# Streamed tiles at 96 and 224 instead of 64 bytes behind the weights, and down projections in written order

## The chip, the cores and the metric

The kernel runs on one core of a Trainium2 chip. The metric is the device time of one execution in microseconds (us). Engines are named as the profile names them: PE multiplies matrices, PEld is its loading of weights, DVE, ACT and POOL work on tiles, SP issues the transfers.

## What is computed

A decoder trunk over 512 tokens of width 1024: two layers, each a mixer and a gated convolutional feed-forward network, with an RMS norm ahead of each and one at the end. The first mixer is dilated window attention (three groups of eight heads), the second a Mamba-2 scan.

```python
for i in range(DEPTH):                       # 2
    h = rmsnorm(x, mix_norm_w[i])
    x = x + (dilated_attention_mixer(h, ...) if i % 2 == 0 else ssd_mixer(h, ...))
    h = rmsnorm(x, ffn_norm_w[i])
    x = x + conv_ffn(h, ffn_w_up[i], ffn_conv_w[i], ffn_conv_b[i], ffn_w_down[i])
return rmsnorm(x, final_norm_w)

def conv_ffn(h, w_up, conv_w, conv_b, w_down):
    u = causal_depthwise_conv(h @ w_up, conv_w, conv_b)
    gate, up = u[..., :D_FF], u[..., D_FF:]           # 2816 each
    return (jax.nn.silu(gate) * up) @ w_down
```

## The kernel before

Activations lie transposed: a tile has 128 features on the partitions and the 512 tokens along the free dimension, so it takes 2048 bytes of each partition. Every dense product is split in two parts for accuracy. A value's high part is the value cast to float32r, its low part what is left. `mm3` (L131) then does three matmuls for one block of 128 x 128 weights: high weights with the high activations, high weights with the low activations, low weights with the high activations. Each is a weight load of 128 columns (512 bytes of each partition) and a stream of 512 columns. The stream does not run straight through its tile: `in_turns` (L122) reads four values (16 bytes), steps 64 bytes on, does so 32 times, and makes four such turns.

A weight unit is 128 x 1024 values: `load_unit` (L106) fetches it into `raw`, ACT casts it to `hi`, and DVE (POOL for the z tiles) subtracts to get `lo`. The buffers of `hi` and `lo` hold 1088 values, which is 4352 bytes or 17 times 256, so all of them begin at the same place modulo 256 bytes. So do the blocks in them, 512 bytes apart, and the streamed tiles, 2048 bytes apart. One number therefore says how the streamed operand lies to the loaded one: the distance of their first bytes modulo 256. The filler tiles `gap` and `gap2`, which nothing uses, set it. It is 64 for each of the 6,504 matmuls with 512 streamed columns and for the 288 with 256.

The streamed tiles are `xh0` to `xh7` and `xl0` to `xl7` (the normed activations), and those that `high_low` makes: attention outputs `o..`, gated units `g..`, scan outputs `y..`. `high_low` takes both parts from one ring of 16 buffers (tag `hl`). For the values of the attention groups 1 and 2 (`v_steps`) the roles are swapped: blocks of `xh` and `xl` are loaded as weights and the weight unit is streamed. There `load_unit` puts the unit 32 values (128 bytes) into its buffer (`at=32`), which again makes the distance 64.

A scheduler orders the instructions of each engine by a timing model of its own, except inside `tc.manual_schedule`, where the written order stands. The mixer of the second layer is written out by hand for PE. The feed-forward network (`ffn`) was left to the scheduler: in three parts (8, 8 and 6 blocks of 128 hidden units) it projects up, gates, and then projects down through `down` (L215), which makes eight output blocks `wd..0` to `wd..7`, each a sum over the part's 8 or 6 gated tiles. `down` writes the product with the last gated tile later than the others (`held`, `finish`), since that tile is made last. Sums lie in three PSUM banks (`mm_bank`), so a fourth block waits until DVE has added the first to the residual `xr`. In the very last part `finish` (L953) works on halves of 256 tokens (`wz..`), norms, and writes the result through output tiles `ot`, which come from the `hl` ring too.

Of the kernel before, what the change touches and what calls it, by code (L numbers as in the profile page):

```python
# [9 lines left out]
F32 = mybir.dt.float32  # L10
F32R = mybir.dt.float32r
# [3 lines left out]
P = 128  # L15
S = 512
D = 1024
KD = D // P
# [33 lines left out]
def trunk(ctx: ExitStack, tc: tile.TileContext, A, out):  # L52
# [4 lines left out]
    cp = ctx.enter_context(tc.tile_pool(name="cp", bufs=1))  # L57
    wr = ctx.enter_context(tc.tile_pool(name="wr", bufs=4))
    wh = ctx.enter_context(tc.tile_pool(name="wh", bufs=5))
    k2 = ctx.enter_context(tc.tile_pool(name="k2", bufs=2))  # L60
# [15 lines left out]
    def t2(name, tag, bufs, pool=k2, dtype=F32):  # L76
        return pool.tile([P, 512], dtype, tag=tag, name=name, bufs=bufs)

    def high_low(name):

        return t2(f"{name}h", "hl", 16, dtype=F32R), t2(f"{name}l", "hl", 16, dtype=F32R)


    par = cp.tile([P, C_END], F32, tag="par", name="par")
# [5 lines left out]

    rcol = cp.tile([P, 4], F32, tag="rcol", name="rcol")
    xh = [cp.tile([P, S], F32R, tag=f"xh{k}", name=f"xh{k}") for k in range(KD)]
    xl = [cp.tile([P, S], F32R, tag=f"xl{k}", name=f"xl{k}") for k in range(KD)]
    rbc = cp.tile([P, S], F32, tag="rbc", name="rbc")

    cp.tile([P, 48], F32, tag="gap", name="gap")
    k2.tile([P, 16], F32, tag="gap2", name="gap2", bufs=1)
    dma(par[:, :C_FFN], A["par"][:, :C_FFN])
    V.memset(ones, 1.0)
    V.memset(mhalf, -0.5)  # L100
# [8 lines left out]
    def load_unit(src, name, n=1024, pieces=1, low=V, at=0):  # L109
        raw = wr.tile([P, 1024], F32, tag="raw", name=f"raw_{name}")  # L110
        hi, lo = (wh.tile([P, 1088], F32R, tag=t, name=f"{t}_{name}")[:, at : at + 1024] for t in ("hi", "lo"))
        for i in range(pieces):
            s = slice(i * n // pieces, (i + 1) * n // pieces)
            dma(raw[:, s], src[:, s])
            if i < pieces - 1:
                V.tensor_copy(hi[:, s], raw[:, s])
            else:
                SC.copy(hi[:, s], raw[:, s])  # L118
            low.tensor_tensor(lo[:, s], raw[:, s], hi.bitcast(F32)[:, s], op=ALU.subtract)  # L119
        return hi, lo  # L120
# [5 lines left out]
    def long_product(dst, w, x, first, last):  # L126
        T.matmul(in_turns(dst), w, in_turns(x), start=first, stop=last)  # L127

    def mm3(dst, hi, lo, at, rh, rl, first, last):
        w_h = hi[:, at * P : (at + 1) * P]  # L130
        w_l = lo[:, at * P : (at + 1) * P]  # L131
        long_product(dst, w_h, rh, first, False)
        long_product(dst, w_h, rl, False, False)
        long_product(dst, w_l, rh, False, last)
# [77 lines left out]
            )  # L212
        return p

    def down(n, load, ms, operand, kn, done, width=512, depth=1):  # L215

        held = []

        def finish():
            m, p, hi, lo, at = held.pop(0)  # L220
            mm3(p, hi, lo, at + kn - 1, *operand(kn - 1), kn == 1, True)
            done(m, p)

        for m in ms:
            hi, lo, at = load(m)
            p = mm_bank(f"{n}{m}")[:, :width]
            for c in range(kn - 1):
                mm3(p, hi, lo, at + c, *operand(c), c == 0, False)
            if len(held) == depth:
                finish()  # L230
            held.append((m, p, hi, lo, at))
        while held:
            finish()
# [4 lines left out]
    def v_steps(g, half, pieces=1):  # L238

        state = {}  # L240
        n = f"v{g}{half}"

        def load(u):
            if u not in state:
                state[u] = load_unit(A["wv"][((g - 1) * 2 + half) * 4 + u], f"{n}{u}", pieces=pieces, at=32)
            return state[u]

        def step(u, bs=(0, 1)):
            if u == 0:
                state["p"] = [mm_bank(f"{n}{j}") for j in range(3)] + [aux_bank(f"{n}3")]  # L250
            hi, lo = load(u)
            for j in range(4):
                js = slice(j * P, (j + 1) * P)
                for b in bs:
                    k = 2 * u + b
                    cs = slice(b * 512, (b + 1) * 512)
                    p = state["p"][j]
                    long_product(p, xh[k][:, js], hi[:, cs], k == 0, False)
                    long_product(p, xl[k][:, js], hi[:, cs], False, False)
                    long_product(p, xh[k][:, js], lo[:, cs], False, k == KD - 1)  # L260
            if u == 3 and bs[-1]:
                tiles = []
                for j in range(4):
                    v = t2(f"{n}_{j}", "v", 12, s3)
                    SC.activation(v, state["p"][j], AF.Copy, scale=rcol[:, j : j + 1])
                    tiles.append(v)
                vt[g, half] = tiles

        return load, [lambda *bs, u=u: step(u, *bs) for u in range(4)]
# [3 lines left out]
    load, first = v_steps(1, 0, 2)  # L273
# [260 lines left out]
    def ffn(layer, done):  # L534
        for part, (c0, cn) in enumerate(FF_PARTS):
            gh, gl = [], []
            for c in range(c0, c0 + cn):
                ab = []
                for gu in range(2):
                    i = 2 * c + gu  # L540
                    n = f"u{layer}_{i}"
                    p = project(A["wup"][layer * 44 + i], n)
                    us = t2("us" + n, "us", 3, lp)
                    V.tensor_tensor(us, p, rbc, op=ALU.mult)  # L544
                    a = t2("a" + n, "a", 13, lp)
                    conv(a, us, C_FCW + (layer * 44 + i) * 3, C_FCB + layer * 44 + i, 3)
                    ab.append(a)
                SC.activation(ab[0], ab[0], AF.Silu)

                by = V if layer == 1 and c == NFF - 1 else G  # L550
                by.tensor_tensor(ab[1], ab[0], ab[1], op=ALU.mult)  # L551
                g_h, g_l = high_low(f"g{c}")
                SC.copy(g_h, ab[1])
                by.tensor_tensor(g_l, ab[1], g_h.bitcast(F32), op=ALU.subtract)
                gh.append(g_h)
                gl.append(g_l)
            n = cn * P

            def load(m):
                i = (layer * len(FF_PARTS) + part) * KD + m  # L560
                return (*load_unit(A["wdn"][i][:, :n], f"wd{i}", n), 0)

            def add(m, p):
                V.tensor_tensor(xr[m], xr[m], p, op=ALU.add)  # L564
                if part == len(FF_PARTS) - 1:
                    done(m)

            if layer == 1 and part == len(FF_PARTS) - 1:
                finish(load, lambda c: (gh[c], gl[c]), cn)
                return  # L570
            down(f"wd{layer}{part}", load, range(KD), lambda c: (gh[c], gl[c]), cn, add)

    def up_first(layer):
        return [(A["wup"][layer * 44 + i], f"u{layer}_{i}") for i in range(3)]
# [383 lines left out]
    def finish(load, operand, cn):  # L958
        for hf in range(2):
            ts = slice(hf * 256, (hf + 1) * 256)  # L960
            ssum = t2(f"ssum4{hf}", "ssum", 2)[:, 0:256]
            last = {}

            def add(m, p):
                x = xr[m][:, ts]
                V.tensor_tensor(x, x, p, op=ALU.add)
                if m < KD - 1:
                    square(m, x, ssum)
                else:
                    last["sq"] = t2("sq", "sq", 2)[:, 0:256]  # L970
                    SC.activation(last["sq"], x, AF.Square)
                w = t2(f"xw{m}", "a", 13, lp)[:, 0:256]
                SC.activation(w, x, AF.Copy, scale=col(C_FIN + m))
                last[m] = w

            down(f"wz{hf}", load, range(KD), lambda c: [t[:, ts] for t in operand(c)], cn, add, 256, 2 - hf)
            rc = sm.tile([P, 2], F32, tag="rc", name="rc", bufs=2)
            inv_rms(ssum, D, rc, last["sq"])
            p = along_free(rc, "rb")[:, 0:256]
            SC.copy(rbc[:, ts], p)  # L980
            for k in range(0, KD, 2):
                ot = t2("ot", "hl", 16)
                for i in range(2):
                    o = ot[:, i * 256 : (i + 1) * 256]
                    if k + i in (1, 4, 7):
                        G.tensor_tensor(o, last[k + i], rbc[:, ts], op=ALU.mult)
                    else:
                        V.tensor_tensor(o, last[k + i], p, op=ALU.mult)
                queue = nc.sync if k % 4 == 0 else nc.scalar
                queue.dma_start(out[k : k + 2, :, ts].rearrange("k p t -> p k t"), ot.rearrange("p (k t) -> p k t", k=2))  # L990
# [103 lines left out]
```

## Time and profile before

| | |
|---|---|
| Median of three runs | 1667.94 us (1667.35 to 1669.39) |
| The profiled execution | 1668.99 us |
| its span, first to last instruction | 1667.2 us |
| Granted clock of PE over the span | 0.998 |
| Matmuls with 512 streamed columns | 6,504 of 8,230 records |
| Weights fetched, HBM read in all | 162.01 MB |

The span is what the views of the trace cover; 1.8 us of the execution lie outside it. A matmul's record (384 ns in the mean for those of the up projections) overlaps the next one's, so how fast a row of matmuls goes is read from the chain of waits instead: it gives, in order of time, stretches of one kind of work with their length and count, and length over count is the spacing. The view by windows gives each engine's busy time in a stage.

### The profile page before, as it was taken

How to read it: one execution, taken by the hardware profiler on the slowest of the kernel's cores; microseconds unless marked ns; L12 is line 12 of the kernel's file. 1: busy time of each engine (PE TensorE's matmuls, PEld its weight loads, DVE VectorE, ACT ScalarE, POOL GpSimd, SP SyncE). 2: the span in 40 equal slices, each digit the busy share in tenths (PEclk: the TensorE clock that was granted, in tenths of full speed). 3: DMA queues.
4: the chain of work that ended last, by engine and by line, in shares of the span. 5: the costliest groups of instructions: out<-in, count | busy, mean ns of one | idle time of the engine just before them, and what ended most of it. 6: DMA issues, size and time to landing. Idle time of an engine off the chain costs nothing.

```text
span 1667.2 us, 21490 instructions
## 1 busy us (share of the span) xinstructions
PE 1648.6 (99%) x8230; PEld 1400.2 (84%) x8230; DVE 1072.1 (64%) x1796; ACT 665.4 (40%) x1000; POOL 464.3 (28%) x303
## 2 busy tenths in 40 slices
PE   9999999999999999999999999999989999999997
PEld 8888888888888888888888888888878888888887
DVE  5366555366658745745666888887787684574565
ACT  5233332333244423433445545454443542342345
POOL 0443443144404210220232232333230331121023
PEclk9999999999999999999999999999999999999999
DMA  7322222222223323233233333322332232332323
GB/s 252 102 77 75 82 84 89 89 76 89 76 89 127 101 88 114 90 100 101 76 114 116 102 101 102 114 75 103 101 102 78 87 113 88 102 101 89 110 74 120
DMA packets 52342, 165.56 MB, mean 99 GB/s; under 512 B 5840, under 2 KB 8144, under 8 KB 52240
## 3 DMA queue, kind: packets, MB, share of 16 engines
q1 hardware_dynamic: 51152, 163.15, 29.6%
q8 instruction: 65, 1.06, 0.3%
q10 hardware_dynamic: 1088, 1.05, 0.2%
q14 instruction: 37, 0.30, 0.1%
HBM read 162.01 MB, written 2.16 MB: 98 GB/s over the span
## 4 chain that ended last, share of the span: by engine, by line
PE 87%; DVE 7%; ACT 3%; issue 2%; DMA 1%; POOL 0%; SPq 0%; POOLq 0%; ACTq 0%; DVEq 0%
PE u L127 28%; PE qk L127 15%; PE wd L127 12%; PE v L127 8%; PE wso L127 4%; PE z L127 3%; PE xs L127 3%; PE wz L127 2%; PE wo L127 2%; DVE axs L529 1%; PE b L127 1%; PE c L127 1%; PE pp L416 1%; PE pg L429 1%; PE po L424 1%
## 5 line engine op out<-in xcount | busy, mean ns | idle before, releaser
L127 PE MATMUL u<-xl,hi_u 128*128 128x512 f32 x704 | 270.0, 384 | 0.4 <-DVE xl L176 0.4
L127 PE MATMUL u<-xh,hi_u 128*128 128x512 f32 x704 | 270.4, 384 | 0.0
L127 PE MATMUL u<-xh,lo_u 128*128 128x512 f32 x704 | 270.0, 384 | 0.0
L551 POOL TENSOR_TENSOR au<-au,au 128x512 f32<-128x512 f32 x43 | 56.7, 1320 | 427.0 <-DVE au L529 406.4
L118 ACT CAST hi_u<-raw_u 128x1024 fp32r<-128x1024 f32 x88 | 91.1, 1043 | 193.9 <-PE u L127 102.1
L529 DVE SCALAR_TENSOR_TENSOR au<-usu,par,au 128x510 f32<-128x510 f32 (+1 forms) x176 | 160.8, 918 | 5.9 <-ACT au L527 1.0
L331 POOL TENSOR_TENSOR rotqk<-rotqk,sr 32x512 f32<-32x512 f32 x48 | 91.9, 1914 | 258.1 <-DVE rotqk L330 215.0
L127 PEld LDWEIGHTS u<-xl,hi_u 128*128 128x128 f32 x704 | 131.9, 187 | 25.9 <-DVE xl L176 0.8
L127 PEld LDWEIGHTS u<-xh,lo_u 128*128 128x128 f32 x704 | 131.9, 187 | 25.4
L127 PEld LDWEIGHTS u<-xh,hi_u 128*128 128x128 f32 x704 | 131.9, 187 | 25.2
L127 PE MATMUL qk<-xh,hi_qk 128*128 128x512 f32 x384 | 149.3, 389 | 0.0
L127 PE MATMUL qk<-xl,hi_qk 128*128 128x512 f32 x384 | 148.4, 387 | 0.0
L127 PE MATMUL qk<-xh,lo_qk 128*128 128x512 f32 x384 | 147.2, 383 | 0.0
L544 DVE TENSOR_TENSOR usu<-u,rbc 128x512 f32<-128x512 f32 x88 | 60.5, 690 | 113.3 <-PE u L127 103.9
L119 DVE TENSOR_TENSOR lo_u<-raw_u,hi_u 128x1024 fp32r<-128x1024 f32 x88 | 110.8, 1264 | 24.2 <-ACT hi_u L118 24.2
L564 DVE TENSOR_TENSOR xr<-xr,wd 128x512 f32<-128x512 f32 x40 | 27.3, 687 | 116.8 <-PE wd L127 116.8
L327 DVE TENSOR_TENSOR qk<-qk,cr 128x512 f32<-128x512 f32 x48 | 33.0, 688 | 91.5 <-PE qk L127 91.3
L118 ACT CAST hi_qk<-raw_qk 128x1024 fp32r<-128x1024 f32 x48 | 50.2, 1045 | 100.4 <-PE v L127 50.0
L127 PEld LDWEIGHTS qk<-xh,lo_qk 128*128 128x128 f32 x384 | 72.0, 187 | 13.4
L127 PEld LDWEIGHTS qk<-xh,hi_qk 128*128 128x128 f32 x384 | 72.0, 188 | 13.0
L118 ACT CAST hi_wd<-raw_wd 128x1024 fp32r<-128x1024 f32 (+1 forms) x56 | 52.3, 952 | 76.7 <-PE wd L127 39.7
L127 PEld LDWEIGHTS qk<-xl,hi_qk 128*128 128x128 f32 x384 | 72.1, 188 | 12.5
(636 smaller groups left out, 3931.1 us busy)
## 6 DMA issues: line engine op xcount, KB each, us to landing
raw_u<-in_wup SPq DMA_DIRECT2D x88, 512.0 KB, 3.2
raw_qk<-in_wqk SPq DMA_DIRECT2D x48, 512.0 KB, 3.2
raw_wd<-in_wdn SPq DMA_DIRECT2D x32, 512.0 KB, 3.2
raw_wd<-in_wdn SPq DMA_DIRECT2D x24, 384.0 KB, 2.9
raw_xs<-in_win SPq DMA_DIRECT2D x16, 512.0 KB, 3.3
raw_z<-in_win SPq DMA_DIRECT2D x16, 512.0 KB, 3.6
lm<-rows SPq DMA_DIRECT2D x32, 256.0 KB, 5.9
raw_wso<-in_wso SPq DMA_DIRECT2D x16, 512.0 KB, 3.2
```

Source lines behind the costliest of these rows:

```text
L118: SC.copy(hi[:, s], raw[:, s])
L119: low.tensor_tensor(lo[:, s], raw[:, s], hi.bitcast(F32)[:, s], op=ALU.subtract)
L127: T.matmul(in_turns(dst), w, in_turns(x), start=first, stop=last)
L327: V.tensor_tensor(at(t), of(p), of(cr), op=ALU.mult)
L331: G.tensor_tensor(rot[R, :], rot[R, :], sr[R, :], op=ALU.mult)
L416: T.transpose(pp[:, b * P : (b + 1) * P], pr[:, b * P : (b + 1) * P], ident)
L424: T.matmul(po[:, ii], v0[h][:, b * P : (b + 1) * P], pts[i][:, (b - i + 1) * P : (b - i + 2) * P], start=b == max(i - 1, 0), stop=b == i,)
L429: T.matmul(pg[:, ii], vt[g, half][i][:, es], pts[i][:, (g + 1) * P : (g + 2) * P], start=g == 1, stop=g == 2,)
L529: V.scalar_tensor_tensor(dst[:, j:], src[:, : S - j], col(c_w + taps - 1 - j), dst[:, j:], op0=ALU.mult, op1=ALU.add,)
L544: V.tensor_tensor(us, p, rbc, op=ALU.mult)
L551: by.tensor_tensor(ab[1], ab[0], ab[1], op=ALU.mult)
L564: V.tensor_tensor(xr[m], xr[m], p, op=ALU.add)
```

## The change

Four edits go together.

Places. A filler of 128 bytes (`gap1`) is put between `xh7` and `xl0`. `gap` shrinks from 192 to 32 bytes and `gap2` grows from 64 to 96. `high_low` now has two rings of 8 buffers, `high` and `low`, and a filler of 128 bytes (`gap3`) is made between them when it is first called. Worked out from these sizes, a streamed high part is now 96 bytes and a streamed low part 224 bytes behind the loaded weights modulo 256: 4,336 of the 6,504 matmuls have 96, and 2,168 have 224. Tiles of the other pools move by multiples of 32 bytes, among them the operands of transposes (from 192 to 64 modulo 256).

Values. Their weight unit begins 48 instead of 32 values into its buffer (192 bytes), which gives 96 against blocks of `xh` and 224 against blocks of `xl`.

Order. Down projections other than the very last part are inside `manual_schedule` for PE. `down` has a new switch `late`: the first two blocks' last products come when the third block has done three of its own tiles.

Outputs. `ot` comes from the ring `high`, so from 8 buffers in place of 16.

```diff
+    kept = []
     def high_low(name):
-        return t2(f"{name}h", "hl", 16, dtype=F32R), t2(f"{name}l", "hl", 16, dtype=F32R)
+        high = t2(f"{name}h", "high", 8, dtype=F32R)
+        if not kept:
+            k2.tile([P, 32], F32, tag="gap3", name="gap3", bufs=1)
+        kept.append(name)
+        return high, t2(f"{name}l", "low", 8, dtype=F32R)
...
     xh = [cp.tile([P, S], F32R, tag=f"xh{k}", name=f"xh{k}") for k in range(KD)]
+    cp.tile([P, 32], F32, tag="gap1", name="gap1")
     xl = [cp.tile([P, S], F32R, tag=f"xl{k}", name=f"xl{k}") for k in range(KD)]
...
-    cp.tile([P, 48], F32, tag="gap", name="gap")
-    k2.tile([P, 16], F32, tag="gap2", name="gap2", bufs=1)
+    cp.tile([P, 8], F32, tag="gap", name="gap")
+    k2.tile([P, 24], F32, tag="gap2", name="gap2", bufs=1)
...
-    def down(n, load, ms, operand, kn, done, width=512, depth=1):
+    def down(n, load, ms, operand, kn, done, width=512, depth=1, late=False):
...
             for c in range(kn - 1):
+                if late and m == 2 and c == 3:
+                    finish()
+                    finish()
                 mm3(p, hi, lo, at + c, *operand(c), c == 0, False)
-            if len(held) == depth:
+            if len(held) == depth and not (late and m == 1):
                 finish()
...
-                state[u] = load_unit(A["wv"][((g - 1) * 2 + half) * 4 + u], f"{n}{u}", pieces=pieces, at=32)
+                state[u] = load_unit(A["wv"][((g - 1) * 2 + half) * 4 + u], f"{n}{u}", pieces=pieces, at=48)
...
-            down(f"wd{layer}{part}", load, range(KD), lambda c: (gh[c], gl[c]), cn, add)
+            with tc.manual_schedule(engines={mybir.EngineType.PE}):
+                down(f"wd{layer}{part}", load, range(KD), lambda c: (gh[c], gl[c]), cn, add, late=True)
...
-                ot = t2("ot", "hl", 16)
+                ot = t2("ot", "high", 8)
```

On PE, order changes only within the five down projections. At the start of the first one (layer 0, part 0) the scheduler had woven the last gated tile's products (`g7h`, `g7l`) of block `wd000` into block `wd002`. A row names output, streamed tile and weights:

```order
L127 MATMUL wd002_4937<-g0h_4338,hi_wd2_4932 128x4x32x4
L127 MATMUL wd002_4937<-g0l_4339,hi_wd2_4932 128x4x32x4
L127 MATMUL wd002_4937<-g0h_4338,lo_wd2_4933 128x4x32x4
L127 MATMUL wd000_4877<-g7h_4867,hi_wd0_4872 128x4x32x4
L127 MATMUL wd002_4937<-g1h_4387,hi_wd2_4932 128x4x32x4
L127 MATMUL wd002_4937<-g1l_4388,hi_wd2_4932 128x4x32x4
L127 MATMUL wd002_4937<-g1h_4387,lo_wd2_4933 128x4x32x4
```

The same place on PE after the change, from the third block's third tile on:

```order
L134 MATMUL wd002_4937<-g2h_4469,hi_wd2_4932 128x4x32x4
L134 MATMUL wd002_4937<-g2l_4470,hi_wd2_4932 128x4x32x4
L134 MATMUL wd002_4937<-g2h_4469,lo_wd2_4933 128x4x32x4
L134 MATMUL wd000_4881<-g7h_4869,hi_wd0_4876 128x4x32x4
L134 MATMUL wd000_4881<-g7l_4870,hi_wd0_4876 128x4x32x4
L134 MATMUL wd000_4881<-g7h_4869,lo_wd0_4877 128x4x32x4
L134 MATMUL wd001_4909<-g7h_4869,hi_wd1_4904 128x4x32x4
L134 MATMUL wd001_4909<-g7l_4870,hi_wd1_4904 128x4x32x4
L134 MATMUL wd001_4909<-g7h_4869,lo_wd1_4905 128x4x32x4
```

The late products now stand in whole groups of high, low, high, block `wd001` right behind `wd000`.

The second place is POOL at the end of the program, where the first half's outputs (`ot`, L986) and the second half's sum of squares (`ssum41`) share the queue. Before, with what each row waits for:

```order
L986 TENSOR_TENSOR ot_13023<-xw1_12867,rbc_98 128x256 [waits Activation_49]
L986 TENSOR_TENSOR ot_13031<-xw4_12960,rbc_98 128x256 [waits PE_49]
L986 TENSOR_TENSOR ot_13035<-xw7_13008,rbc_98 128x256 [waits PE_49]
L186 TENSOR_TENSOR ssum41_13039<-ssum41_13039,sq_13179 128x256 [waits Activation_49,Pool_49]
L186 TENSOR_TENSOR ssum41_13039<-ssum41_13039,sq_13210 128x256 [waits Activation_49,Pool_49]
```

And after the change:

```order
L997 TENSOR_TENSOR ot_13040<-xw1_12884,rbc_99 128x256 [waits Activation_49]
L193 TENSOR_TENSOR ssum41_13056<-ssum41_13056,sq_13196 128x256 [waits Activation_49,Pool_49]
L997 TENSOR_TENSOR ot_13048<-xw4_12977,rbc_99 128x256 [waits DMAHW5_49,DVE_49,Pool_49]
L997 TENSOR_TENSOR ot_13052<-xw7_13025,rbc_99 128x256 [waits DMAHW6_49,DVE_49,PE_49]
L193 TENSOR_TENSOR ssum41_13056<-ssum41_13056,sq_13227 128x256 [waits Activation_49,Pool_49]
```

The third and fourth output tile of the first half now reuse the buffers of the first and second and wait for their transfers out (`DMAHW5`, `DMAHW6`); three of the second half's sums stand behind them.

## The prediction

> **What bounds the kernel now.** I read the page first: the engines' shares, then the chain of work that ended last. In a chain row the share is of the span.
>
> ```profile
> PE 1648.6 (99%) x8230; PEld 1400.2 (84%) x8230; DVE 1072.1 (64%) x1796; ACT 665.4 (40%) x1000; POOL 464.3 (28%) x303
> ...
> PE 87%; DVE 7%; ACT 3%; issue 2%; DMA 1%; POOL 0%; SPq 0%; POOLq 0%; ACTq 0%; DVEq 0%
> PE u L127 28%; PE qk L127 15%; PE wd L127 12%; PE v L127 8%; PE wso L127 4%; PE z L127 3%; PE xs L127 3%; PE wz L127 2%; PE wo L127 2%; DVE axs L529 1%; PE b L127 1%; PE c L127 1%; PE pp L416 1%; PE pg L429 1%; PE po L424 1%
> ```
>
> PE is the bound. The products of `mm3` with 512 streamed columns (L127 without `wz`) hold 28 + 15 + 12 + 8 + 4 + 3 + 3 + 2 + 1 + 1 = 77% of the span, 1284 us. How fast they go I then read from the chain in order of time (start, length, what, count), first where nothing else happens:
>
> ```profile
> 597.77 42.88 PE wd L127 x192
> 640.65 85.76 PE u L127 x384
> 726.41 42.88 PE wd L127 x192
> ...
> 1428.99 85.76 PE u L127 x384
> ```
>
> 42.88 / 192 and 85.76 / 384 both give **223.33 ns** from one product to the next, in both layers, up and down. The pieces follow each other without a wait. So 1284 / 0.22333 = some 5,750 of the 6,504 products lie on the chain, and each nanosecond of their spacing is worth 5.75 us. The other 750 lie mostly in the scan of the second layer, where the view by windows (start and end, length, then busy us and count of PE, PEld, DVE, ACT and POOL) shows PE with idle time beside DVE work:
>
> ```profile
> 880.00:1270.00 390.00, 381.90 (x2120) 324.82 (x2119) 312.51 (x553) 188.61 (x276) 107.23 (x71) 1.00 0.32 102
> ```
>
> There PE is busy 381.9 of 390 us and DVE 312.5; a quicker product there only makes PE wait longer for DVE, and I count nothing for those 750.
>
> Is 223.33 the fastest such a product can go? Other stretches of the chain, all of them at the same distance of 64 bytes:
>
> ```profile
> 30.04 21.14 PE v L127 x96
> ...
> 149.70 14.25 PE qk L127 x64
> ...
> 93.61 6.54 PE qk L127 x29
> ```
>
> They give 220.2, 222.7 and 225.5 ns. The spacing settles into one of several patterns, and which one depends on how the row of products began; the 29 at 93.61 us follow a restart behind other work and had not settled. Fastest of all are the score matmuls, which stream 256 columns of fp32 and come two records each:
>
> ```profile
> 194.44 0.43 PE sc L373 x2
> 194.88 0.22 PE sc L374 x2
> ```
>
> 0.43 / 2 is 215 ns for a record, 8.3 ns under the 223.33 (and 110 ns for the records with 128 columns). That is the nearest row for a full stream that is held up by nothing.
>
> **The change part by part.** *Places (the main term).* No instruction is added or removed; 6,504 streams start elsewhere relative to the weights that are loaded beside them. The trace has no product at 96 or 224, so the price is bounded by rows: at best 215 ns, so 8.3 x 5.75 = 48 us less; at worst the spacing of the unsettled 29, 225.5 ns, so 2.2 x 5.75 = 12.5 us more. Within these the patterns give steps. 220.0, 446.7 (two of 223.33) and 1113.3 (five of 222.66) are 33, 67 and 167 times 6.67 ns: every settled pattern closes on a multiple of that. Now the distances run 96, 224, 96 within each block of weights, so I expect a pattern that closes over three products, and its mean can only be 217.8, 220.0, 222.2, 224.4 or 226.7 ns. I take 220.0 to 220.2, since it is the one of these that the trace shows, and holds for 96 products without a break: 223.33 - 220.21 = 3.12 ns, times 5,750 is **17.9 us less**. What makes the spacing at all I cannot show from this trace; that it varies by 5 ns at one distance says that it is set by how stream and load fall on each other in time, which their places may shift.
>
> [...]
>
> *Halves of the last part.* Its products stream 256 columns:
>
> ```profile
> 1628.33 14.18 PE wz L127 x120
> ```
>
> 118.2 ns each, 288 of them. Between 110 ns (the 128-column records above are the nearest row without delay) and some 2 ns more, that is 2.4 us less to 0.6 us more. I take 0: their own row stands for them, since nothing says which way they go.
>
> *Transposes.* Their operands move from 192 to 64. The chain has them as
>
> ```profile
> 175.47 0.44 PE pp L416 x4
> 175.91 0.45 PE po L424 x4
> ```
>
> 110 ns for a transpose (pp) and 112 for a matmul at distance 0 (po). Some 240 transposes at 2 ns more or less are 0.5 us; I take 0.
>
> *Written order.* In the quiet stretches above the 192 products of a down projection take 42.88 us, no more than as many of the up projection, so there is nothing in the order to be won. Only the third part of layer 0 shows something: 32.25 us for 144 (a row of the chain, then two of the timeline, where a row starts with start and length and ends with the idle time before it).
>
> ```profile
> 833.61 32.25 PE wd L127 x144
> ...
> 838.99 1.28 POOL L554 TENSOR_TENSOR g21l<-au,g21h 128x512 fp32r<-128x512 f32 x1 [0.73 <-ACT g21h L553]
> ...
> 844.81 1.28 DVE L564 TENSOR_TENSOR xr<-xr,wd 128x512 f32<-128x512 f32 x2 [7.98 <-PE wd L127]
> ```
>
> That is 223.96 each, 0.09 us over 144 x 0.22333. The fourth block there waits for the first one's bank until DVE has added it. In written order the first block is finished sooner, nine products (2.0 us) before the fourth starts, against one DVE addition of 0.64 us, so this wait goes; what comes next is an ordinary product. The new order needs `g21l` about 1.8 us earlier, at some 842.4 us; POOL has it at 840.3. In parts 0 and 1 the last gated tile is needed no earlier. Cover is gone only if the last gated tile were 2 us late, and then PE would wait for that much three times. Deferred additions stand ahead of `lo` work on DVE; DVE is busy 64% of the span, and the weights are cast several units ahead. I take 0 for the order, between 0.5 us less (five projections of 0.1) and 1 us more.
>
> *Output ring.* Two products of the first half on POOL now wait for transfers, and three sums stand behind them (two rows of the timeline, and the transfers' row, whose last number is the time to landing):
>
> ```profile
> 1650.60 12.21 SPq L990 DMA_DIRECT2D out<-ot  x4
> ...
> 1656.10 0.73 POOL L186 TENSOR_TENSOR ssum<-ssum,sq 128x256 f32<-128x256 f32 x1 [0.88 <-ACT sq L185]
> ...
> out<-ot SPq DMA_DIRECT2D x4, 256.0 KB, 2.7
> ```
>
> The first tile leaves at 1650.6 us and lands 2.7 us on, at 1653.3. Two products of 0.7 us follow, to 1654.7, then three sums of 0.73: the last ends at 1656.9, where it now ends at 1656.8. The wait hides in POOL's idle time. DVE's part of these tiles holds the additions of `wz` up by about 1 us, behind which PE has other blocks' work. I take 0.1 us, so 0, and at most 1 us.
>
> *Sum.* 1667.2 - 17.9 = 1649.3 us of span; with the 1.8 us around it 1651.1, against 1668.99 for this execution. Its own time is 1.05 us over the median of the three runs, so the forecast on the median is 1667.9 - 17.9 = **1650.0 us**.
>
> **The rivals.** *Deeper (0.17).* The three distances fall so that the pattern closes at 217.8 ns: 5.55 x 5.75 = 31.9 us less, 1636 us; at the floor of 215 ns it would be 1620. For it: the score rows. Against it: no row of `mm3` settles there.
>
> *Shallower (0.17).* 222.2 ns, near the five-product pattern of 222.7 that `qk` shows: 1.1 x 5.75 = 6.5 us less, 1661.5 us.
>
> *Places have no say (0.13).* The 8.3 ns over the floor come from something that the distance does not touch, or the edit shifts all patterns alike. [...] Time: 1667.9 us, with the order's 0.5.
>
> *Slower (0.25).* One mechanism: with distances that alternate 96, 224, 96 the row of products never settles, and each is spaced as just after a restart. The place is every stretch of `mm3`, the price that of the 29 products, 225.5 ns, so 12.5 us more: 1680.4 us. It decides when the mean spacing goes over 223.9 ns (223.33 and 0.2% of the time, 3.3 us over 5,750). For it: a pattern at 224.4 is as possible as one at 222.2, and the long runs at 223.33 show that the slower settled pattern is where most rows end. Against it: 223.33 is the slowest pattern that holds for long here.
>
> That the change does not do what it says can be left out: the places follow from sizes, and the order on PE has been compared row by row.
>
> **How the numbers follow.** The forecast case (near 220 ns, 1646 to 1655 us) has 0.28 and is the likeliest; with the deeper and the shallower one, faster has 0.62. No change within 0.2%, about what a measurement of this kernel can tell from none, has 0.13, and slower 0.25. The range runs from just under the deeper pattern (1634) to just over the unsettled price (1681); outside lie the floor of 215 and a spacing over 225.5, together about 0.15.
>
> **What would show it.** In the chain of the changed kernel, 192 products of a down projection should take 42.2 to 42.3 us, and 384 of an up projection 84.5. 42.88 again means that places have no say; 43.1 or more means slower; 41.8 the deeper pattern. The scan should keep its length, with PE idle for longer in it. The third part of layer 0 should have no product that is late by 0.1 us at the fourth block. At the end POOL's last sum should come within 0.3 us of the last addition of the seventh block. I would be wrong if the scan shortened with the products (then 750 products more count, 2.3 us), or if the gain stood in some stages and not in others, because attention restarts its rows every few microseconds and the feed-forward network hardly ever does.

## The result, and the profile after

The changed kernel takes 1659.08 us (median of four runs, 1658.33 to 1659.21) where the kernel before takes 1668.66 (1667.35 to 1670.15): a ratio of 0.9938, with a 95% interval from 0.9927 to 0.995. That is 9.6 us less by the medians, and 10.7 us by the two profiled executions (1668.99 and 1658.33 us, spans 1667.2 and 1656.5). I had forecast 17.9 us less. The time lies between the forecast case (1646 to 1655 us) and the shallower rival (1661.5 us). The direction came true, and so did the 220 ns of the long rows; the size did not, and the experiments show that my word for the cause, "places", says only half of it.

The page of the changed kernel, as before: PE bounds it, and the shares of its chain are within a point of the earlier ones.

```profile
PE 1637.6 (99%) x8230; PEld 1400.3 (85%) x8230; DVE 1070.4 (65%) x1796; ACT 665.6 (40%) x1000; POOL 462.7 (28%) x303
...
PE 87%; DVE 7%; ACT 3%; issue 1%; POOL 1%; DMA 1%; POOLq 0%; ACTq 0%; DVEq 0%
```

The chain of the changed kernel in order of time (start, length, what, count), in the two feed-forward networks:

```profile
596.07 42.24 PE wd L134 x192
638.31 84.48 PE u L134 x384
722.79 42.24 PE wd L134 x192
...
1421.18 84.48 PE u L134 x384
```

42.24 / 192 and 84.48 / 384 are 220.00 ns each, where 223.33 stood: the pattern that I had picked from the list. The starts of single matmuls in the trace come 217, 222 and 221 ns apart, over and over: 660 ns for three, 99 times 6.67.

The same chain in the prologue and the attention of layer 0:

```profile
29.62 21.32 PE v L134 x96
50.94 32.99 PE qk L134 x144
...
103.98 14.08 PE qk L134 x64
```

Here the gain is uneven. The 64 products of `qk` went from 222.7 to 220.0 ns. But the 144 in a row at the start went to 229.1 ns, and the 96 of `v` from 220.2 to 222.1. The chain of the kernel before has those 144 at 223.3:

```profile
51.17 32.16 PE qk L127 x144
```

So at the pair of distances 96 and 224 a slow pattern holds as well: starts 236, 227 and 224 ns apart, 687 for three, 103 times 6.67.

By stages, from the starts in the trace. The first stage begins with PE's first matmul, 1.05 us into the span; the others begin with the first `qk`, the first scores `sc`, the first `u` of layer 0, the first `wdt`, the first matmul of the scan proper (`pd`), the first `u` of layer 1 and the first `wz`:

| stage | before, us | after, us | difference |
|---|---|---|---|
| start to the first `qk` | 49.96 | 49.73 | -0.23 |
| first `qk` products | 37.52 | 38.49 | +0.97 |
| attention, output projection | 420.90 | 419.44 | -1.46 |
| feed-forward of layer 0 | 356.26 | 351.21 | -5.05 |
| first projections of layer 1 (`wdt`) | 17.93 | 18.72 | +0.79 |
| scan | 410.71 | 409.80 | -0.91 |
| feed-forward of layer 1, to the halves | 327.46 | 322.67 | -4.79 |
| halves and end | 45.43 | 45.40 | -0.03 |

The two feed-forward networks gain 9.84 us; everything else together gains 0.87.

### The profile page after: what moved, and what is told of

The parts are those of the page before. It is cut to its first block, busy times and chain, and to the rows that moved or that the text cites. A ratio compares the mean times of both kernels' runs of the same rounds, so it can differ in the third digit from the quotient of the medians.

```text
span 1656.5 us, 21492 instructions
## 1 busy us (share of the span) xinstructions
PE 1637.6 (99%) x8230; PEld 1400.3 (85%) x8230; DVE 1070.4 (65%) x1796; ACT 665.6 (40%) x1000; POOL 462.7 (28%) x303
## 3 DMA queue, kind: packets, MB, share of 16 engines
q10 hardware_dynamic: 1088, 1.05, 0.2%
## 4 chain that ended last, share of the span: by engine, by line
PE 87%; DVE 7%; ACT 3%; issue 1%; POOL 1%; DMA 1%; POOLq 0%; ACTq 0%; DVEq 0%
PE u L134 28%; PE qk L134 15%; PE wd L134 12%; PE v L134 8%; PE wso L134 4%; PE z L134 3%; PE xs L134 3%; PE wo L134 2%; PE wz L134 1%; DVE axs L539 1%; PE b L134 1%; PE c L134 1%; PE pp L426 1%; PE pg L439 1%; PE po L434 1%
## 5 line engine op out<-in xcount | busy, mean ns | idle before, releaser
L134 PE MATMUL u<-xl,hi_u 128*128 128x512 f32 x704 | 266.4, 378 | 0.4 <-DVE xl L183 0.4
```

## The experiments

The spacing of a row, below, is the mean difference of the starts of its matmuls. A row is called settled when its differences repeat. Three theories stood at the start. P: the pair of distances sets the spacing that a row of products settles into. O: the written order of the down projections brings the gain. N: neither does; something else moved along. A fourth, E, came up on the way.

**Places alone.** The change without its written order:

```diff
-            with tc.manual_schedule(engines={mybir.EngineType.PE}):
-                down(f"wd{layer}{part}", load, range(KD), lambda c: (gh[c], gl[c]), cn, add, late=True)
+            down(f"wd{layer}{part}", load, range(KD), lambda c: (gh[c], gl[c]), cn, add)
```

> The change without its written order (the scheduler orders the down projections again); places, values and output ring as in the change. Theory P (places set the spacing, order gives nothing): 192 products of a down projection take 42.2 to 42.5 us, 384 of an up projection 84.5; the wait of PE on xl at the start of the second layer's first product (0.6 us in the change) goes, so 1658 to 1659 us, ratio to before 0.993 to 0.995. Theory O (the written order, whole groups of high, low, high, is what lets the 220 ns pattern hold): down projections 42.6 us or more and the products behind them too, 1661 us or more.

Measured: 1656.29 us (1655.73 to 1657.91), ratio 0.9929 [0.9916, 0.9941]. The whole gain is there without the written order; the time is 1.7 us under the forecast of P. The chain of this kernel:

```profile
1376.74 42.27 PE wd L134 x192
1419.01 84.48 PE u L134 x384
```

**Written order alone.** The kernel before with `manual_schedule` and `late` from the change, all distances at 64.

> The kernel before with the written order of the down projections alone; all places at 64 bytes. Theory P: 42.88 us for 192 products as before, 1668 to 1669 us, ratio 0.999 to 1.001, and the PE wait of about 0.6 us on xl at the second layer's start shows here too. Theory O: less than 42.7 us, 1664 us or less.

Measured: 1669.62 us (1667.85 to 1670.73), ratio 1.0004 [0.9996, 1.0013]: nothing won. The chain keeps its 223.33 ns, and the view of PE's waits (engine and line that waits, for whom, us in total, times, longest) has a row that the kernel before lacks:

```profile
597.00 42.88 PE wd L127 x192
639.88 85.76 PE u L127 x384
```

```profile
PE wdt L127 <- DVE xl L176: 0.5, 1, 0.5
```

O falls. The new wait is a cost of the written order: `down` still holds the last blocks' closing products of layer 0's last part back, DVE adds them late, and the low part `xl7`, for which `wdt` is the first to wait, comes late (0.5 us here). The changed kernel has the same row:

```profile
PE wdt L134 <- DVE xl L183: 0.6, 1, 0.6
```

**Closing in time.** The change, with the last three blocks of that part closed at once:

```diff
+            if late and kn == 6 and m > 4:
+                while held:
+                    finish()
```

> The change, with the last three blocks of layer 0's last down projection closed at once and not one block later. If the late closing of the seventh block is what makes PE wait 0.6 us on xl, that wait goes and the time is 0.5 to 1.0 us under the change's, 1658.3 us. If the wait has another cause (DVE's queue as such), it stays and so does the time, 1659.1 us.

Measured: 1657.09 us (1656.6 to 1658.35), ratio 0.9933 [0.992, 0.9947]. The wait is gone, and the stage of `wdt` has 17.89 us instead of 18.72 (before: 17.93). In the whole time the 0.8 us are smaller than the intervals.

**A map of pairs.** A bare kernel of rows of 48 products; each row has another pair of distances, behind four transposes or behind score-like matmuls:

```python
for h in range(0, 64, 8):          # high part, 32 bytes a step
    for l in range(0, 64, 8):      # low part
        ...
        xh, xl = x[0][:, h : h + S], x[1][:, l : l + S]
        product(mm, hi[:, ks], xh, ...); product(mm, hi[:, ks], xl, ...); product(mm, lo[:, ks], xh, ...)
```

> A kernel of its own that computes none of the reference: 128 rows of 48 products as in mm3, two rows for each of 64 pairs of distances (high 0 to 224, low 0 to 224, in steps of 32 bytes), one row behind four transposes and one behind four score-like matmuls. Theory P: the settled spacing (last 24 products) depends on the pair: 223.3 (or 220.0 or 222.7) at 64/64, 220.0 at 96/224, and others between 217 and 230, each a multiple of 6.67 ns over the products of its pattern; at 96/224 the first ten products after the restart cost more than at 64/64. Theory N (places have no say): the same spacing for all 64 pairs within 0.5 ns, but for the kind of restart.

Measured, mean of the last 18 spacings of a row in ns (a part of the 64 pairs, high/low):

| pair | behind transposes | behind scores |
|---|---|---|
| 64/64 (before) | 223.3 | 223.3 |
| 96/224 (the change) | 220.0 | 220.0 |
| 96/64 | 220.0 | 220.0 |
| 128/64 | 221.1 | 221.1 |
| 32/64 | 222.2 | 222.2 |
| 64/128 | 226.7 | 220.0 |
| 32/32 | 225.2 | 220.0 |
| 96/160 | 231.1 | 231.1 |

The same instructions settle anywhere from 220.0 to 231.6 ns, and nowhere under 220.0. N falls in its plain form. But 64/128 and 32/32 have two answers, by what stood ahead of the row, and so have others of the 64 pairs (64/32: 229.3 and 222.2), which P has no place for.

**Another good pair.** 96/64, in the scheduler's order (fillers `gap1`, `gap3` of 56 values, `gap` of 48, values again at 32; a filler behind the rings keeps the other tiles where they were):

> High parts at 96, low parts at 64 (instead of 224), values at 32 and 64, scheduler's order in the down projections as in the run with places alone (1656.29 us). Theory P (the pair of distances sets the spacing that a row of products settles into; the gain comes only from long rows): the map of pairs gives 220.0 ns settled for 96/64 too, so 192 products of a down projection again take 42.24 us and 384 of an up projection 84.48 us; the feed-forward networks keep their gain of 9.8 us. The map also has this pair lower over the first 18 products behind transposes (222.3 against 225.5 ns for 96/224), so the attention should be shorter by 1 to 3 us, less 384 value products at 222.2 instead of 220 (0.8 us): 1653 to 1657 us in all. Rival N (it is not the pair but something else that moved with it): then the spacing is not 220.0, 42.88 us or more for 192 products, and the time returns to 1663 us or over.

Measured: 1657.16 us (1656.09 to 1659.35), ratio 0.9931 [0.9918, 0.9945]. As P has it, 384 up products take 84.48 us; 192 down products take 42.41, a little over its 42.24. The first 144 `qk` products are quick here (that stage takes 37.01 us instead of 38.49), but the attention behind them is 0.9 us longer than with places alone, so the shorter start that the map promised is not to be had in the sum.

**A bad pair.** 96/160 (`gap1` and `gap3` of 16 values, `gap` of 24, a filler of 16 behind the rings):

> High parts at 96, low parts at 160, all else as in the run with places alone, values at 96 and 32. Theory P: the map gives 231.1 ns settled (row of 48 products) in either kind of start, 11.1 ns over 220.0, so 192 products of a down projection take 44.37 us and 384 of an up projection 88.74; against the 221.2 ns mean of the run with places alone it is 9.9 ns more for 5,750 products, 57 us, and up to 64 us if the scan's 750 count too: 1711 to 1721 us. Rival N (places have no say in the whole kernel): within 1656 to 1668 us. Rival M (the map's price holds only in bare rows; casts, subtractions and transfers beside the products blur it): half of it or less, under 1690 us.

Measured: 1696.96 us (one run), 28 us over the kernel before and outside all three forecasts. The chain says why:

```profile
531.07 72.06 PE u L137 x321
...
647.20 88.74 PE u L137 x384
735.94 44.29 PE wd L137 x192
```

The 384 take 231.1 ns each, as in the map; the 321 products of the first stretch, at the same pair, take 224.5. In the attention the mean (of spacings up to 260 ns) is 227.3. So the bad pair slows the whole kernel, but not every row by the map's price: this pair, too, has two settled patterns. That the beginning of a row decides between them is a guess here; the rows with seeds, below, test it.

**The rings alone.** The kernel before with `high` and `low` rings at 96/224; normed activations stay at 64/64, so up projections have nothing moved (`gap2` 24 values, a filler behind the rings).

```diff
-        return t2(f"{name}h", "hl", 16, dtype=F32R), t2(f"{name}l", "hl", 16, dtype=F32R)
+        high = t2(f"{name}h", "high", 8, dtype=F32R)
+        if not kept:
+            k2.tile([P, 32], F32, tag="gap3", name="gap3", bufs=1)
+        low = t2(f"{name}l", "low", 8, dtype=F32R)
...
```

> The kernel before with the two rings alone (gated units, attention outputs, scan outputs and output tiles at 96/224, output tiles from 8 buffers); normed activations stay at 64/64. Theory P: the down projections settle at 220.0 ns (192 products 42.24 us), the up projections keep 223.33 (384 products 85.76 us); the stretch from the first up product of layer 0 to the second layer shortens by 528 x 3.33 ns = 1.8 us at most, that of layer 1 by 384 x 3.33 = 1.3 us, everything else as before: 3 us less in all, about 1665 us beside 1668.5. Rival: if the gain came from the output ring or from tiles that only the rings move, the up projections would change too, or the whole 10 us would show here.

Measured: 1661.07 us (one run, so the argument rests on the chain), 4 us under what P gives. The chain, with the first up stretch of layer 0 and what follows it:

```profile
524.60 71.69 PE u L136 x321
596.28 42.28 PE wd L136 x192
638.56 84.49 PE u L136 x384
```

The first 321 up products run at 223.3 ns, as before. Behind the first down projection, which runs at 220.2, the next 384 up products run at 220.0, though they lie at 64/64 as they always did. Their starts are an even 220 ns apart, not 217, 222, 221: it is another pattern, of the old pair. It was there to be seen before the change: the 96 products of `v` at 220.2 ns, from which I took my number, are an even 220 ns apart too. This made theory E: a pair of distances has several settled patterns, and the products ahead of a row pick one.

**Entries.** A bare kernel again: a seed of 3, 6, 12 or 48 products at one of four pairs, directly followed by 48 at one of the four.

> A kernel of its own, computes none of the reference: 128 rows of products; each row starts with a seed of 3, 6, 12 or 48 products at one pair of distances (64/64, 96/224, 96/64, 96/160), directly followed by 48 products at a second pair, behind four transposes or four score-like matmuls. It asks whether the pair alone sets the settled spacing (theory P), or the pair sets which patterns there are and the products ahead pick one (theory E, formed on the run with the rings alone, where up products at 64/64 kept 220.0 ns behind down products that ran at 220.0). P: the last 18 products of 64/64 take 223.3 ns behind every seed, those of 96/160 231.1, those of 96/224 and 96/64 220.0. E: 64/64 takes 220.0 behind a seed of 12 or 48 products at 96/224 that has settled at 220.0, and 223.3 behind a seed at 64/64; 96/160 takes 224.4 to 224.6 behind some seeds (as in the first up products of layer 0 in the run at 96/160) and 231.1 behind others; 96/224 may keep more than 220.0 behind a seed at 96/160.

Measured, rows by the spacing of their last 18 products (32 rows for each pair: four seed pairs, four lengths, two kinds of start):

| pair of the 48 | settled spacing in ns: rows |
|---|---|
| 64/64 | 220.0: 15, 223.3: 12, others to 233.3: 5 |
| 96/224 | 220.0: 30, 228.9: 2 |
| 96/64 | 220.0: 29, 226.7: 3 |
| 96/160 | 224.4: 12, 231.1: 20 |

Behind 6, 12 or 48 products at 96/224, 64/64 keeps 220.0 in every row; behind a seed at 64/64 it keeps 223.3 in every row. E holds and P falls as I had it. One thing that E allowed for did not come: behind 96/160 every row at 96/224 is at 220.0. What sets 96/224 and 96/64 apart is that nearly every entry here led to 220.0 (30 and 29 rows of 32, against 15 at 64/64 and none at 96/160).

**Activations alone.** The run with places alone, with the rings back at 64/64 (no `gap3`; `gap2` 16 values, a filler of 40 behind the rings). Now nothing is moved in the down projections.

> The run with places alone, but with the rings (gated units, attention and scan outputs) back at 64/64: only the normed activations stand at 96/224, and the values' units at 192 bytes. Theory P (pair alone): down products settle at 223.33 ns, so 192 take 42.88 us, up products at 220.0 (84.48 us for 384); against the run with places alone (1656.29 us) 912 down products lose 3.0 us: about 1659.3 us, ratio 0.9944. Theory E (entry picks among the patterns of a pair): down products that follow up products settled at 220.0 keep 220.0 also at 64/64, 42.24 us for 192, and the time is that of the run with places alone, 1656.3 us, ratio 0.993.

Measured: 1659.74 us (1658.41 to 1660.16), ratio 0.9935 [0.9919, 0.9952]. The median lies at P's 1659.3 us, but the interval holds E's 0.993 as well as P's 0.9944, so the total cannot tell them apart; the chain can:

```profile
1379.22 42.25 PE wd L135 x192
1421.47 84.58 PE u L135 x384
```

The down projections at 64/64 take 220.05 ns behind up products at 220.0. So with the rings moved the up projections behind them come along (220.0 ns), and with the normed activations moved the down projections do (220.05).

**A map of units.** Rows of 24 products at 64/64, then one unit of 24 with its high and low weights up to 224 bytes further on, then 48 at 64/64 again:

> A kernel of its own, computes none of the reference: 64 rows of 24 products at 64/64, then 24 (one weight unit) whose high and low weights stand 0 to 224 bytes further on in their buffers (all pairs of steps of 32 bytes), then 48 at 64/64 again. Theory E (each pair of distances has several settled patterns, and the products ahead pick one): without a shift the last 18 products keep 223.3 ns; behind some of the 63 shifted units they take 220.0 though nothing stands elsewhere any more, behind others 223.3 or a third spacing above it, and each spacing holds to the end of the row without creeping back. Rival T (what stood behind the seeds was a slow transient, not a second settled pattern): all rows are back at 223.3 in their last 18 products.

Measured: 20 of the 63 shifted units leave the row at 220.0 ns, 40 at 223.3, 3 at another spacing (222.4, 222.7, 228.1), always to its end. T falls. A shift of the low weights alone by 32 bytes is one of the 20. The row without a shift was the first of the program and ran at 220.0 from its start, so it is no control; the rows of 64/64 behind 64/64 in the run with seeds are.

Two of its units also show that the distance counts, and not where the stream lies by itself: in the map of pairs the streams were moved, here the weights. With both weights 32 bytes on (distances 32/32) the unit's starts are 219, 230, 224, 232 and 222 ns apart, over and over, as in the map of pairs at 32/32 behind transposes. With both 192 bytes on (distances 128/128 modulo 256) they are 225, 234, 234 and 227 ns apart, as at 128/128 behind scores.

**One unit shifted.** The kernel before, and of its 6,504 products 16 moved: the low weights of the sixth up unit of each layer.

```diff
-        hi, lo = (wh.tile([P, 1088], F32R, tag=t, name=f"{t}_{name}")[:, at : at + 1024] for t in ("hi", "lo"))
+        hi, lo = (
+            wh.tile([P, 1088], F32R, tag=t, name=f"{t}_{name}")[:, b : b + 1024]
+            for t, b in (("hi", at), ("lo", at + shift))
+        )
...
-                    p = project(A["wup"][layer * 44 + i], n)
+                    p = project(A["wup"][layer * 44 + i], n, shift=8 if i == 5 else 0)
```

> The kernel before, all streamed tiles at 64/64, with one thing moved: the low weights of one up unit of each layer (the sixth, 8 products of 704 times 3) stand 32 bytes further on in their buffer. Theory E: in the map of units this shift left the row at 220.0 ns; if the sixth unit's start falls on the same phase here, all up and down products behind it in the feed-forward network keep 220.0 ns: about 1,430 products of layer 0 and 1,270 of layer 1 at 3.33 ns less, 9.0 us, so 1659.5 us beside 1668.5; 192 products of a down projection 42.24 us. If the phase is another (20 of the map's 63 shifts worked, so the chance for a layer is no more than a half), that layer keeps 223.33 and the gain of its half (4.8 or 4.2 us) is missing. Theory P (the pair of a product alone sets its spacing): 16 products in 6,504 have moved, nothing is to be seen: 1668.5 us, 42.88 us for 192.

Measured: 1659.93 us (1659.32 to 1661.02), ratio 0.9948 [0.9932, 0.9965].

```profile
525.89 70.88 PE u L130 x321
596.77 42.24 PE wd L130 x192
639.01 84.48 PE u L130 x384
...
1422.18 84.48 PE u L130 x384
```

220.0 ns in both layers. In layer 0 the starts are 222 and 225 ns apart up to the sixth unit's first product, unsettled within that unit, and at 220 from the seventh on. They stay there to the halves in layer 1, and in layer 0 to the last down projection. There the fourth block starts late, and behind it the spacing is back at 223.3 ns (a row of the chain, then three of the timeline):

```profile
829.09 32.15 PE wd L130 x144
...
840.59 0.39 PE L130 MATMUL wd<-g21h,lo_wd 128*128 128x512 f32 x1
840.87 0.50 PE L130 MATMUL wd<-g16h,hi_wd 128*128 128x512 f32 x1
841.21 0.38 PE L130 MATMUL wd<-g16l,hi_wd 128*128 128x512 f32 x1
```

The run with activations alone loses the pattern at the same place (281 and 336 ns, then 223.3). The run with places alone has a late fourth block too (249 and 329 ns), but at 96/224 it is back at 220.0 after about ten products. This is a single case, but it is what the rows with seeds let one expect (30 of 32 rows at 96/224 at 220.0).

The feed-forward stages take 351.87 and 323.08 us, within 0.7 us of the change, and the attention keeps its 420.97. Both layers took the good entry, where I had given each no more than a half. The other entry, 96 bytes (`shift=24`), does the same:

> As the run before it, with 96 instead of 32 bytes for the same two units' low weights. The map of units has 220.0 ns behind this shift as well, by another way into it; the same two outcomes for each layer: 220.0 ns from the seventh unit to the end of the feed-forward network, 4.8 us (layer 0) and 4.2 us (layer 1) less, or 223.33 and nothing. Theory P: nothing, 1668.5 us.

Measured: 1660.86 us (1660.57 to 1662.3), ratio 0.9953 [0.9939, 0.9968].

```profile
1381.63 42.24 PE wd L130 x192
1423.87 84.48 PE u L130 x384
```

Here too both layers came out at 220.0. No version stands clearly ahead of the change: places alone has the lowest median, and the interval of its ratio overlaps with that of the change.

## Why the prediction was right in direction and wrong in size

**The bound and the pattern: right.** PE stayed the bound, and the step "a pattern that closes over three products" at 220.0 came out as 217 + 222 + 221 ns. It was a choice among five, taken because the trace showed 220.2 for 96 products; it was no derivation. That row was at 64/64 and in another pattern (an even 220 ns), and 96/224 can also hold at 229.1, so that the number came out is in part luck.

**The count: the step that was mis-sized.** The term was 5,750 products x 3.12 ns = 17.9 us. Of its 77 points of the chain, 40 are `u` and `wd`: 2,987 products, 9.3 us of the forecast. They gave 9.84 us. The other 2,763 (8.6 us) gave 0.87, with the 0.8 us that the written order cost (below) already taken off. Counting them at all took each as settled and as on the path that sets the end. Three things stood against that, which the differences of the starts of matmuls show:

- In the attention the mean of the spacings up to 260 ns fell from 223.41 to 221.57 ns over 1,461 products, 2.7 us. But there the seven rows of 64 products are at 220.02 in the mean, those of 20 products and fewer at 223.03 (before, 224.33): of the 18 `qk` products from 171.8 us on, 13 of the 17 spacings come before the pattern of 220.0 begins. And 1.2 us came back at the 48 places where another kind of matmul follows a product: it starts 253.5 ns behind it in the mean, where it was 228.2. Why it does is not settled.
- The first `qk` stretch fell into the slow pattern: 1.0 us more.
- In the scan the mean of the spacings up to 260 ns fell from 224.01 to 221.60 ns, 3.4 us over 1,398 products, but the stage fell by 0.91 us only. Gaps over 260 ns are 45 instead of 36, and another kind of matmul behind a product (27 places, 345.0 instead of 317.6 ns) costs 0.7 us more. The quicker products are not the only cause of the gaps: the run with the written order alone has 46 of them, at 64/64. The stage itself takes 409.97 and 411.44 us in the two runs with one unit shifted, whose scans are the same program, so 0.91 us is within what it varies by. I had said that the scan keeps its length and set aside 750 products for it; but `z`, `xs`, `wso`, `b` and `c`, 12 points of the 77, are scan products too, and I had counted those 900. The window that I had quoted, in the changed kernel (start and end, length, busy us and count of PE, PEld, DVE, ACT, POOL):

```profile
880.00:1270.00 390.00, 381.84 (x2122) 326.85 (x2121) 314.79 (x557) 189.63 (x278) 105.13 (x69) 0.99 0.31 99
```

2,122 matmuls where 2,120 were, at the same 390 us (which begin 5.0 us further on in the program): quicker products did not make the scan quicker by their count. I had put that down to DVE, which no run shows: the view of PE's waits has 8.1 us for the scan both before (`wso` for DVE 6.0, `prg` for POOL 2.1) and after (5.8 and 2.3). Slower products do show, since at 96/160 the stage takes 415.09 us. What sets its pace stays open.

I had named this outcome among the things that would prove me wrong ("if the gain stood in some stages and not in others, because attention restarts its rows every few microseconds"), and yet gave the sum the full count.

**Halves and transposes: right.** `wz` has its old row:

```profile
1617.64 14.18 PE wz L134 x120
```

A transpose (`pp`) takes 110 ns as before and a matmul of `po` 112:

```profile
476.38 0.44 PE pp L426 x4
476.81 0.45 PE po L434 x4
```

**Written order: inside its bounds, with the value taken wrong.** I took 0, between 0.5 us less and 1 us more; it costs 0.8 us in the stage of `wdt`. The fourth block of layer 0's last part is no longer late, as I had said (before, its first two products came 272 and 326 ns behind the one ahead, 0.15 us too much and not 0.09; after, no start comes more than 240 ns behind). I looked for the late addition's victim among the down projections; it was `xl7` in the next layer's first projection.

**Output ring: 0, as forecast, but not by the cover that I named.** The chain of the changed kernel now runs through the ring:

```profile
1639.89 2.60 DMA out<-ot
...
1642.69 1.25 POOL ot L997 x2
...
1645.67 0.73 POOL ssum L193
```

The last sum ends at 1646.40 us. The timeline of the changed kernel (start, length, engine, line, operation, idle time before it) has the additions of the seventh and the eighth block:

```profile
1644.33 0.42 DVE L977 TENSOR_TENSOR xr<-xr,wz 128x256 f32<-128x256 f32 x1 [0.29 <-PE wz L134]
...
1646.42 0.42 DVE L977 TENSOR_TENSOR xr<-xr,wz 128x256 f32<-128x256 f32 x1 [1.67 <-PE wz L134]
```

and that of the kernel before, too:

```profile
1655.03 0.42 DVE L966 TENSOR_TENSOR xr<-xr,wz 128x256 f32<-128x256 f32 x1 [1.66 <-PE wz L127]
...
1657.12 0.42 DVE L966 TENSOR_TENSOR xr<-xr,wz 128x256 f32<-128x256 f32 x1 [1.67 <-PE wz L127]
```

The last sum comes 1.65 us behind the seventh addition, where it came 1.38 behind it before (1656.83 against 1655.45). So "within 0.3 us of the last addition" was a wrong mark, as the profile of before could have told. It is still done when the eighth block's addition begins, at 1646.42, and the end waits for the square of that: the halves and the end take 45.40 us, before 45.43. To that mark POOL had 0.29 us to spare before (1657.12 less 1656.83), and has 0.02 now. But the addition does not wait for POOL; PE does, which sums POOL's tile and then the square. Its idle time ahead of the square is the room that is left, 0.61 us before and 0.34 now:

```profile
1658.11 0.61 PE L196 MATMUL ss<-ones,sq 128*128 128x1 f32 x4 [0.61 <-ACT sq L971]
```

```profile
1647.40 0.61 PE L203 MATMUL ss<-ones,sq 128*128 128x1 f32 x4 [0.34 <-ACT sq L982]
```

**The rivals.** *Places have no say* fell: 96/160 and 96/224 differ by 11.1 ns with the same instructions. But what spoke for it, that the trace of before has several spacings at the one distance of 64 (220.2, 222.7 and 223.3 ns), so that distance alone does not set them, was the better half of the truth: 16 products moved by 32 bytes bring 8.8 us in the feed-forward stages (356.26 - 351.87 and 327.46 - 323.08). *Slower* came near in the `qk` stretch alone, and there as a row that settles in a slow pattern (229.1 ns), not as one that never settles. The 29 products of its price settle too: in the trace of before the starts of that row are 225 and 222 ns apart, over and over, from the 13th spacing on. *Shallower* gave 1661.5 us, near the 1659.08 measured, but not in the way it came about: the long rows are at 220.0 and other stages gave little. (Its 6.5 us should read 6.4, 1.11 x 5.75.) *Deeper* fell: no row of these products in the bare kernels, and no long one in the whole kernels, settled under 219.9 ns.

**What stays open.** That the spacing is set by how stream and load fall on each other in time was my guess. The runs show that it goes with the distances and with the products ahead; what falls together inside the chip, so that the patterns here close on multiples of 6.67 ns (660, 687, 920 and 1127 ns), no run shows, nor why a given entry leads to a given pattern. A shift of one unit was not tried together with the change, nor against the slow `qk` stretch or in the attention, where the rows may be too short for it.

## What to carry to other kernels

Count a gain in spacing only for rows that are long enough to settle and that set the end: read it by stages, with the start differences of one row each, before multiplying by a share of the chain. Where a long row of equal matmuls settles over its best pattern, look at what starts it: a shift of 32 bytes in one weight tile at the head of the row did nearly as much here for the feed-forward networks (8.8 us) as the whole change (9.84). Which pattern a row settled into depended here on the products ahead of it (at 64/64, 15 rows of 32 came to 220.0 ns and 12 to 223.3), so it is worth checking again after any edit ahead of it.

## What the runs showed of the hardware that was not expected

- One pair of places has several steady patterns that last for 168 to over a thousand products: 64/64 has 220.0 (even starts) and 223.3 ns, 96/160 has 224.4 and 231.1, 96/224 has 220.0 and 229.1 (228.9 in two rows with seeds).
- The pattern is handed on. In the run with one unit shifted, 192 + 384 + 192 + 288 products of layer 0 at 64/64 follow each other at 220.0 ns without a slip, between up and down projections too; two late products (280 and 337 ns) end it.
- A restart costs more than its first late product: in the map of pairs a row at 96/224 behind four transposes needs 12 more products, at a mean of 228 ns, before it settles at 220.0; behind score matmuls it settles at once. At 64/64 it is the other way about: it settles at 223.3 at once behind transposes, after 11 more behind score matmuls.
